# A hybrid encoder block in fp32 halves: one shared ring of half pieces for landed weights, sums and low parts

## The chip, the cores and the metric

The kernel runs on one core of one Trainium2 chip. The metric is the device time of one execution in microseconds (us), as a median of several runs. A profiled execution gives the trace from which the rows below come.

## The reference, cut to what matters

One layer of an encoder on 256 tokens of width 2048, in fp32. `w_in` has 10240 columns, the MLP is 5632 wide.

```
h = rms_norm(x, attn_norm)
proj = h @ w_in                       # q, k, v of branch A; q, k, v of branch B; gates ga, gb
ya = windowed_gqa(qa, ka, va)         # 8 heads
yb = dilated_attention(qb, kb, vb)    # 12 heads in three patterns, merged to 4
merged = sigmoid(ga) * (ya @ w_branch_a) + sigmoid(gb) * (yb @ w_branch_b)
x = x + merged @ w_out
hf = rms_norm(x, ffn_norm)
g = dwconv_centred(hf @ w_ffn_gate, conv_w, conv_b)      # three taps over the tokens
x = x + (gelu(g) * (hf @ w_ffn_up)) @ w_ffn_down
x = x + sigmoid(rms_norm(x, ple_norm) @ w_ple_gate) * (p @ w_ple_proj)
out = rms_norm(x, final_norm)
```

## The kernel before, in words

All weights lie in HBM as pieces of 128 x 2048 fp32 (1 MB), in the order of use: 258 pieces. Each product is done to nearly fp32 precision in parts: a weight `w` is rounded to a high part `hi` (ScalarE, a copy to the type fp32r, L264) and a low part `lo = w - hi` (VectorE, L265), the activations likewise, and TensorE multiplies the parts. `block` and `unit_blocks` (L292, L308 and L293, L315) have the weights as the stationary operand: a matmul of 512 columns with `hi` (both parts of the activations side by side) and one of 256 columns with `lo`. `thirds` (L365 to L367) has the activations stationary and three matmuls of 512 columns.

A *unit* is the part of a piece that is rounded in one go, mostly half a piece (1024 columns). `produce` makes the next unit: it asks for the pieces up to two ahead (`load`, on SP's DMA queue, into the ring `raw` of three whole pieces), then rounds the unit. Units go into rings: six pairs `uh`, `ul`, and, for sums, two pairs `vh`, `vl`. When TensorE's last instruction on a unit is issued, `drop` frees it and `pump` produces more while a ring has room. A planner orders the instructions of each engine by its own costs and the order of the program; `keep` pins an instruction to the order of the program. Every buffer's reuse is a wait on whoever used it last.

The stages, in order: A (projections and attention: stationary weights), then for j = 0 to 3 the gates B*j* with the branch products `ba`*j* and `bb`*j*, D0 and D1 (`w_out`), E0 (gate and up of the first half of the MLP), F00 and F01 (its part of `w_ffn_down`), E1, F10 and F11, `pp0` and `pp1` (the embedding), and G0, G2, G3 (its gate). E is stationary weights; B, D, F and G0 are *quad stages*: two 512-column halves by two token halves by pairs of contraction chunks. A piece of a quad stage is `s` (eight products, each three matmuls) or `S`, in which seven products take the place of eight, as in Strassen's and Winograd's scheme: M1 to M7, on sums of the activations (`combos`, `sums_of`) and on four sums of the weights. For an `S` piece `produce` wrote the sums in place on the landed piece, with one VectorE operation of 1024 columns and two of 512 (L257 to L259), after both plain units had been rounded; the units `T13` and `T24` are the sums'. Patterns such as "SsSsSsSs" give the pieces of a stage. At the end of a quad stage `row_sums` adds the banks up (L823 to L826), and the residual rows are updated and squared (L936, L938, L940).

In stage E, `mlp` works on one chunk of 128 MLP columns at a time, as its accumulator ends: `gather` adds the two halves of the accumulator (L456, L460); for a gate chunk the norm, three taps and the gelu's polynomial and tanh (L981 to L989), for an up chunk the product with the gelu and the split into high and low parts (L995 to L997).

The last product, G3, is two pieces taken together (`joint`), and its last two contraction chunks of the second token half are done by halves of 256 columns (`ends`), so that the first half of the bank is complete earlier. Then come the rows' tanh, residual, squares and the final norm (L1106 to L1122), and the output's DMAs.

Of the kernel before, what the change touches and what calls it, by code (L numbers as in the profile page):

```python
# [10 lines left out]
F32 = mybir.dt.float32  # L11
FR = mybir.dt.float32r
AF = mybir.ActivationFunctionType
ALU = mybir.AluOpType
# [73 lines left out]
WARM = 11  # L88
JOINT = 4
JOINED = 2  # L90
# [8 lines left out]
def _ffn(half):  # L99

    jobs = []
    for f in range(FHALF + 1):
        if f < FHALF:
            jobs.append(("g", half * FHALF + f))
        if f:
            jobs.append(("u", half * FHALF + f - 1))
    return jobs
# [52 lines left out]
_PIECES, _STAGES = _pieces()  # L160
_NPIECES = len(_PIECES)
# [22 lines left out]
RINGS = {"u": 6, "v": 2}  # L184
# [3 lines left out]
def _encoder(ctx: ExitStack, tc, xt, pt, xrow, cols, gainrow, table, onehot, mask, ident_in, wts, out):  # L188
# [42 lines left out]
    def tap(i, f):  # L231
# [5 lines left out]
    raws, made = {}, {}  # L237
    state = {"raw": 0, "unit": 0, "at": 0, "early": True,
             "u": RINGS["u"], "v": RINGS["v"]}

    def load(r, a=0, b=PIECE):
        if a == 0:
            raws[r] = wpool.tile([P, PIECE * P], F32, name="raw", bufs=3)
        nc.sync.dma_start(raws[r][:, a * P:b * P], wts[r][:, a * P:b * P])
        state["raw"] = r + 1

    def produce():

        u = state["unit"]
        p, kind, a, b = _UNITS[u]  # L250
        while state["raw"] < min(p + 3, _NPIECES):
            load(state["raw"])
        raw = raws[p]
        ring = "u" if kind == "n" else "v"
        if kind == "T13":
            q = [raw[:, i * WIDE:(i + 1) * WIDE] for i in range(4)]
            nc.vector.tensor_tensor(raw[:, :2 * WIDE], raw[:, WIDE:3 * WIDE], raw[:, :2 * WIDE], op=ALU.subtract)  # L257
            nc.vector.tensor_tensor(q[2], q[2], q[0], op=ALU.subtract)
            nc.vector.tensor_tensor(q[3], q[3], q[2], op=ALU.subtract)  # L259
        src = raw[:, a:b]  # L260
        pool = wpool if ring == "u" else held["tok"]
        hi = pool.tile([P, b - a], FR, name=ring + "h", bufs=RINGS[ring])
        lo = pool.tile([P, b - a], FR, name=ring + "l", bufs=RINGS[ring])
        nc.scalar.activation(hi, src, AF.Copy)  # L264
        nc.vector.tensor_tensor(lo, src, hi.bitcast(F32), op=ALU.subtract)  # L265
        made[u] = (hi, lo)
        state["unit"] = u + 1
        state[ring] -= 1

    def pump():  # L270
        while not state["early"] and state["unit"] < len(_UNITS):
            p, kind = _UNITS[state["unit"]][:2]
            if state["u" if kind == "n" else "v"] <= 0 or kind != "n" and "tok" not in held:
                break
            produce()
# [6 lines left out]
    def drop(u):  # L282
        del made[u]
        state["u" if _UNITS[u][1] == "n" else "v"] += 1
        pump()
# [76 lines left out]
    def thirds(acc, stationary, w, first, last):  # L362

        (sh, sl), (wh, wl) = stationary, w
        nc.tensor.matmul(acc, sh, wh, start=first, stop=False, skip_group_check=True)  # L365
        nc.tensor.matmul(acc, sh, wl, start=False, stop=False, skip_group_check=True)  # L366
        nc.tensor.matmul(acc, sl, wh, start=False, stop=last, skip_group_check=True)  # L367
# [4 lines left out]
    def quad_stage(stage, moving, combos=None, tags=("M2", "M3", "M4", "P22")):  # L372
# [24 lines left out]
        for i, p in enumerate(pieces):  # L397
            kind = _PIECES[p][0]
            us = _UNITS_OF[p]
            a, b = moving(2 * i), moving(2 * i + 1)  # L400
            if kind == "s":
                for g in range(8):
                    run_due(stage, i, g)
                    t, n, c = g // 4, g // 2 % 2, g % 2
                    w = cut(us[c], n if c == 0 else 1 - n)
                    put(tags[2 * t + n], part((a, b)[c], t), w)
                drop(us[0])
                drop(us[1])
            else:
                s = combos(i)  # L410
                sums = [(s[:, 0, e], s[:, 1, e]) for e in range(4)]
                for g, (name, stationary, u, c, gone) in enumerate((
                        ("M1", part(a, 0), 0, 0, 0), ("M7", sums[2], 2, 1, None), ("M5", sums[0], 2, 0, 2),
                        ("M6", sums[1], 3, 0, None), ("M2", part(b, 0), 1, 1, None), ("M3", sums[3], 1, 0, 1),
                        ("M4", part(b, 1), 3, 1, 3))):
                    run_due(stage, i, g)
                    put(name, stationary, cut(us[u], c))
                    if gone is not None:
                        drop(us[gone])
        return accs  # L420

    def wide_stage(stage, moving, names, joint=1):
# [3 lines left out]
        ends = []  # L426
        alone = len(pieces) - joint
        for i, span in [(i, 1) for i in range(alone)] + [(alone, joint)]:
            g = 0
            for t in range(2):  # L430
                for c in range(4 * span):
# [11 lines left out]
            for h in range(2) if ends else ():  # L443
                for e, (stationary, w) in enumerate(ends):
                    cs = slice(h * T, (h + 1) * T)
                    thirds(accs[1][:, cs], stationary, [a[:, cs] for a in w], False, e == 1)
            if ends:
                drop(_UNITS_OF[pieces[-1]][1])
# [84 lines left out]
    tot = ap_.tile([P, T], F32, name="tot", bufs=1)  # L533
# [11 lines left out]
    for step in order:  # L545
        if len(step) == 3:
            load(*step)
        elif step[0]:
            cs = slice(KC + step[0] * T, KC + step[1] * T)
            nc.sync.dma_start(flat[:, cs], xt[:, cs])  # L550
    nc.sync.dma_start(cl, cols)
    nc.sync.dma_start(ident, ident_in)
    nc.sync.dma_start(oh, onehot)
    nc.sync.dma_start(tb, table)
    nc.sync.dma_start(mk, mask)
# [13 lines left out]
    for step in order:  # L569
# [9 lines left out]
        while 4 * done + 5 < state["at"] // FIRST:  # L579
            square(done)  # L580
            done += 1
# [4 lines left out]

    for i in range(2):
        first_gather(i)
# [384 lines left out]

    def mlp(kind, n, acc):
        tok = held["tok"]
        if kind == "g":
            if n % 2 == 0:
                held["gw"] = tok.tile([P, 4, T], F32, name="gw", tag="c%d" % (n // 2 % 2 + 1))
            c, w = (held["gw"][:, 2 * (n % 2) + i] for i in range(2))
            u = gather(acc)  # L980
            nc.vector.tensor_tensor(u, u, rt[1], op=ALU.mult)  # L981
            nc.vector.tensor_scalar(c, u, tap(1, n), tap(3, n), op0=ALU.mult, op1=ALU.add)
            nc.vector.scalar_tensor_tensor(c[:, 1:], u[:, :-1], tap(0, n), c[:, 1:], op0=ALU.mult, op1=ALU.add)
            nc.vector.scalar_tensor_tensor(c[:, :-1], u[:, 1:], tap(2, n), c[:, :-1], op0=ALU.mult, op1=ALU.add)
            nc.scalar.activation(w, c, AF.Square)
            nc.vector.tensor_scalar(w, w, 0.044715, 1.0, op0=ALU.mult, op1=ALU.add)
            nc.vector.tensor_tensor(w, w, c, op=ALU.mult)
            nc.scalar.activation(w, w, AF.Tanh, scale=GELU_C)
            nc.vector.scalar_tensor_tensor(c, w, 1.0, c, op0=ALU.add, op1=ALU.mult)  # L989
            held["gelu", n] = c  # L990
        else:
            if n % 2 == 0:
                held["pair"] = tok.tile([P, 2, T], F32, name="pair", bufs=2)
            u = gather(acc, u=held["pair"][:, n % 2])
            nc.vector.scalar_tensor_tensor(u, u, 0.5, rt[1], op0=ALU.mult, op1=ALU.mult)  # L995
            nc.vector.tensor_tensor(u, u, held.pop(("gelu", n)), op=ALU.mult)
            halves(activation_row(n), u)  # L997
            pair = n % FHALF // 2
            if n % 2 and DOWN[pair] == "S":
                combos["act", pair] = sums_of(held["pair"], pair // 2)  # L1000
# [101 lines left out]
    for t in range(2):  # L1102
# [8 lines left out]
        nc.vector.tensor_tensor(known[:, t:t + 1], known[:, t:t + 1], ssq[:, t, 3:4], op=ALU.add)  # L1111
        nc.vector.tensor_scalar(v, ssq[:, t, 4:], known[:, t:t + 1], 1.0 / D, op0=ALU.add, op1=ALU.mult)
        r = sc.tile([P, 1], F32, name="r3")
        nc.gpsimd.tensor_tensor(r, v, mhalf[:, :1], op=ALU.pow)
        nc.vector.tensor_tensor(xr[:, t, cut[3]], xr[:, t, cut[3]], gains[:, cut[3]], op=ALU.mult)
# [62 lines left out]
```

## Time and profile before

| | |
|---|---|
| median of 3 runs | 1457.39 us (1457.05 to 1457.96) |
| the profiled execution: its own time | 1457.96 us |
| its span from first to last instruction | 1456.2 us |
| TensorE matmul busy | 1444.5 us, 7488 matmuls |
| VectorE (DVE) busy | 1248.8 us |
| ScalarE (ACT) busy | 822.1 us |
| HBM read | 279.49 MB, 193 GB/s over the span |

In the rows, PE is TensorE's matmuls, PEld its weight loads (they run beside matmuls), DVE VectorE, ACT ScalarE, POOL GpSimd, SP the engine that issues most DMAs. A row of a group has the line, engine, operation, written and read tiles, shapes and count, then busy us, mean ns of one, and the engine's idle time just before. A row of the timeline begins with start and length in us, and ends, where the engine had waited, with for how long and on whom. Matmuls overlap, so the length of one (391 ns for 512 columns) is more than the distance to the next.

### The profile page before, as it was taken

How to read it: one execution, taken by the hardware profiler on the slowest of the kernel's cores; microseconds unless marked ns; L12 is line 12 of the kernel's file. 1: busy time of each engine (PE TensorE's matmuls, PEld its weight loads, DVE VectorE, ACT ScalarE, POOL GpSimd, SP SyncE). 2: the span in 40 equal slices, each digit the busy share in tenths (PEclk: the TensorE clock that was granted, in tenths of full speed). 3: DMA queues.
4: the chain of work that ended last, by engine and by line, in shares of the span. 5: the costliest groups of instructions: out<-in, count | busy, mean ns of one | idle time of the engine just before them, and what ended most of it. 6: DMA issues, size and time to landing. Idle time of an engine off the chain costs nothing.

```text
span 1456.2 us, 19520 instructions
## 1 busy us (share of the span) xinstructions
PE 1444.5 (99%) x7488; PEld 1235.9 (85%) x7488; DVE 1248.8 (86%) x1849; ACT 822.1 (56%) x1141; POOL 4.1 (0%) x9
## 2 busy tenths in 40 slices
PE   9999999999999999999999999999999999999997
PEld 8888888888888888888888888888888888888785
DVE  7677665679998989989888899989888889999995
ACT  7455544446555656666555555455555555565762
POOL 0000000000000000000000000000000000000000
PEclk9999999999999999999999999999999999999999
DMA  9654444535546456465554545565555554546462
GB/s 335 249 206 146 152 168 175 175 141 203 192 187 235 180 213 234 174 232 193 186 199 175 202 152 221 176 254 183 199 184 193 185 192 173 193 191 234 170 237 81
DMA packets 46312, 282.88 MB, mean 194 GB/s; under 512 B 4932, under 2 KB 9668, under 8 KB 13964
## 3 DMA queue, kind: packets, MB, share of 16 engines
q1 hardware_dynamic: 45500, 280.46, 53.2%
q8 instruction: 58, 0.95, 0.3%
q10 hardware_dynamic: 720, 1.19, 0.2%
q14 instruction: 34, 0.28, 0.1%
HBM read 279.49 MB, written 2.14 MB: 193 GB/s over the span
## 4 chain that ended last, share of the span: by engine, by line
PE 97%; DVE 1%; ACT 1%; issue 1%; DMA 0%; SPq 0%; POOL 0%; POOLq 0%; DVEq 0%; ACTq 0%
PE bank L308 29%; PE bank L315 15%; PE bank L365 14%; PE bank L366 14%; PE bank L367 14%; PE bank L354 2%; PE bank L356 2%; PE bank L355 2%; PE bank L292 1%; PE bank L293 1%; PE bank L870 1%; PE bank L687 0%; PE bank L635 0%; PE bank L634 0%; PE bank L633 0%
## 5 line engine op out<-in xcount | busy, mean ns | idle before, releaser
L264 ACT ACTIVATE uh<-raw 128x1024 fp32r<-128x1024 f32 (+2 forms) x518 | 522.3, 1017 | 399.5 <-PE bank L308 183.6
L265 DVE TENSOR_TENSOR ul<-raw,uh 128x1024 fp32r<-128x1024 f32 (+2 forms) x518 | 596.8, 1169 | 128.9 <-ACT uh L264 68.8
L308 PE MATMUL bank<-hf,uh 128*128 128x512 f32 x1408 | 336.3, 391 | 0.0
L308 PEld LDWEIGHTS bank<-hf,uh 128*128 128x128 f32 x1408 | 258.9, 188 | 50.2
L315 PEld LDWEIGHTS bank<-hf,ul 128*128 128x128 f32 x1408 | 180.4, 191 | 6.7
L315 PE MATMUL bank<-hf,ul 128*128 128x256 f32 x1408 | 182.8, 283 | 0.0
L264 ACT ACTIVATE vh<-raw 128x1024 fp32r<-128x1024 f32 x92 | 97.4, 1058 | 57.0 <-DVE raw L257 25.4
L265 DVE TENSOR_TENSOR vl<-raw,vh 128x1024 fp32r<-128x1024 f32 x92 | 111.9, 1219 | 0.4
L308 PE MATMUL bank<-hs,uh 128*128 128x512 f32 x432 | 103.6, 392 | 0.0
L456 ACT ACTIVATE t<-bank 128x256 f32<-128x256 f32 x122 | 46.5, 384 | 96.6 <-PE bank L315 89.5
L308 PEld LDWEIGHTS bank<-hs,uh 128*128 128x128 f32 x432 | 79.5, 188 | 15.6
L365 PE MATMUL bank<-uh,act 128*128 128x512 f32 x232 | 90.4, 390 | 0.0
L366 PE MATMUL bank<-ul,act 128*128 128x512 f32 x232 | 90.4, 390 | 0.0
L367 PE MATMUL bank<-uh,act 128*128 128x512 f32 x232 | 90.3, 389 | 0.0
L365 PE MATMUL bank<-uh,hs 128*128 128x512 f32 x172 | 67.3, 391 | 0.0
L367 PE MATMUL bank<-uh,hs 128*128 128x512 f32 x172 | 67.3, 391 | 0.0
L366 PE MATMUL bank<-ul,hs 128*128 128x512 f32 x172 | 67.1, 390 | 0.0
L257 DVE TENSOR_TENSOR raw<-raw 128x1024 f32<-128x1024 f32 x46 | 56.1, 1221 | 0.6
L315 PE MATMUL bank<-hs,ul 128*128 128x256 f32 x432 | 56.6, 284 | 0.0
L315 PEld LDWEIGHTS bank<-hs,ul 128*128 128x128 f32 x432 | 54.5, 191 | 1.0
L366 PE MATMUL bank<-vl,S 128*128 128x512 f32 x138 | 54.1, 392 | 0.1
L365 PE MATMUL bank<-vh,S 128*128 128x512 f32 x138 | 54.1, 398 | 0.0
(240 smaller groups left out, 2273.2 us busy)
## 6 DMA issues: line engine op xcount, KB each, us to landing
raw<-in_wts SPq DMA_DIRECT2D x251, 1024.0 KB, 4.8
raw<-in_wts SPq DMA_DIRECT2D x12, 512.0 KB, 7.2
xr<-in_xrow SPq DMA_DIRECT2D x4, 512.0 KB, 8.3
x<-in_xt SPq DMA_DIRECT2D x13, 128.0 KB, 6.0
hb<-hold SPq DMA_DIRECT2D x3, 514.0 KB, 5.9
hb<-hold SPq DMA_DIRECT2D x2, 768.0 KB, 7.5
last<-in_gainrow SPq DMA_DIRECT2D x1, 1024.0 KB, 6.9
out<-xr SPq DMA_DIRECT2D x4, 256.0 KB, 2.6
```

The lines of the kernel that those rows point to most:

```text
L257: nc.vector.tensor_tensor(raw[:, :2 * WIDE], raw[:, WIDE:3 * WIDE], raw[:, :2 * WIDE], op=ALU.subtract)
L264: nc.scalar.activation(hi, src, AF.Copy)
L265: nc.vector.tensor_tensor(lo, src, hi.bitcast(F32), op=ALU.subtract)
L308: nc.tensor.matmul(acc, weights(u)[0][:, o * P:(o + 1) * P], m, start=first, stop=False, skip_group_check=True)
L315: nc.tensor.matmul(acc[:, T:], weights(u)[1][:, o * P:(o + 1) * P], m[:, :T], start=False, stop=last, skip_group_check=True)
L354: nc.tensor.matmul(acc[:, :n * P], xh, hi, start=(k == 0), stop=False)
L355: nc.tensor.matmul(acc[:, :n * P], xh, lo, start=False, stop=False)
L356: nc.tensor.matmul(acc[:, :n * P], xl, hi, start=False, stop=(k == KC - 1))
L365: nc.tensor.matmul(acc, sh, wh, start=first, stop=False, skip_group_check=True)
L366: nc.tensor.matmul(acc, sh, wl, start=False, stop=False, skip_group_check=True)
L367: nc.tensor.matmul(acc, sl, wh, start=False, stop=last, skip_group_check=True)
L456: keep(nc.scalar.activation(t, acc[:, T:], AF.Copy, scale=scale))
```

## The change

- The rings `raw`, `uh`/`ul` and `vh`/`vl` go. One ring `w` of twelve tiles of 128 x 1024 (`SPLIT`) holds landed half pieces, the sums of weights, and low parts; a ring `h` of seven (`ROUND`) holds the high parts. Each load is half a piece; `produce` asks for four loads beyond those that it needs (`AHEAD`).
- An `S` piece's units are ordered: first half's plain columns, both units of sums, second half's. Its sums are written by four operations of 512 columns into two tiles of the ring, before its first unit is rounded. M4 is moved ahead of M2 and M3. Code for sums kept in DRAM (`_SUMS_AT`, kind `Z`) is added, and is not used: `_SUMS_AT` is empty.
- `mlp` evacuates each chunk as before, but does everything after that for two chunks at a time, on tiles of 512 columns; the centre tap goes to ScalarE, and the up product of a chunk comes two gate products later instead of one (`LAG`).
- At the start the loads and the chunks of `x` are asked for twelve steps ahead of their use (`EARLY`), not all at once; the squares come four chunks later; `tot` shares the slot of `far`.
- G3 is no longer cut in halves. Three instructions of the last norm are kept in the order of the program.

The core of the diff:

```diff
-    for f in range(FHALF + 1):
+    for f in range(FHALF + LAG):                       # LAG = 2
...
-        elif kind == "S":
-            cuts = [("n", 0, WIDE), ("n", 2 * WIDE, 4 * WIDE), ("T13", 0, 2 * WIDE), ("T24", 2 * WIDE, 4 * WIDE)]
+        elif kind in "SZ":
+            cuts = [("n", 0, WIDE), (kind + "13", 0, 2 * WIDE), (kind + "24", 2 * WIDE, 4 * WIDE),
+                    ("n", 2 * WIDE, 4 * WIDE)]
...
-RINGS = {"u": 6, "v": 2}
+SPLIT, ROUND = 12, 7
+AHEAD = 4
...
+    def load():
+        u, p, half = _LOADS[state["load"]]
+        state["load"] += 1
+        t = wpool.tile([P, 2 * WIDE], F32, name="w", bufs=SPLIT)
...
+        nc.sync.dma_start(t[:, :b - a], src[:, a:b])
+
+    def sums_of_weights(p):
...
+        t, v = (wpool.tile([P, 2 * WIDE], F32, name="w", bufs=SPLIT) for _ in range(2))
...
+        nc.vector.tensor_tensor(s1, q[1], q[0], op=ALU.subtract)
+        nc.vector.tensor_tensor(s2, q[2], s1, op=ALU.subtract)
+        nc.vector.tensor_tensor(s3, q[2], q[1], op=ALU.subtract)
+        nc.vector.tensor_tensor(s4, q[3], s2, op=ALU.subtract)
...
     def produce():
...
-        while state["raw"] < min(p + 3, _NPIECES):
-            load(state["raw"])
...
+        last = us[-1] if _PIECES[p][0] == "S" else u
+        while state["load"] < min(_LOAD_OF[last] + 1 + AHEAD, len(_LOADS)):
+            load()
+        if u == us[0]:
...
+            if _PIECES[p][0] == "S":
+                sums_of_weights(p)
...
+        hi = wpool.tile([P, 2 * WIDE], FR, name="h", bufs=ROUND)[:, :n]
+        lo = wpool.tile([P, 2 * WIDE], FR, name="l", tag="w", bufs=SPLIT)[:, :n]
+        nc.scalar.activation(hi, w, AF.Copy)
+        nc.vector.tensor_tensor(lo, w, hi.bitcast(F32), op=ALU.subtract)
...
-                        ("M1", part(a, 0), 0, 0, 0), ("M7", sums[2], 2, 1, None), ("M5", sums[0], 2, 0, 2),
-                        ("M6", sums[1], 3, 0, None), ("M2", part(b, 0), 1, 1, None), ("M3", sums[3], 1, 0, 1),
-                        ("M4", part(b, 1), 3, 1, 3))):
+                        ("M1", part(a, 0), 0, 0, 0), ("M7", sums[2], 1, 1 - z, None), ("M5", sums[0], 1, z, 1),
+                        ("M6", sums[1], 2, 0, None), ("M4", part(b, 1), 2, 1, 2),
+                        ("M2", part(b, 0), 3, 1, None), ("M3", sums[3], 3, 0, 3))):
...
-                    if 1 < joint == span and t and c >= 4 * span - 2:
-                        ends.append((part(moving(k), t), w))
-                        continue
...
-        while 4 * done + 5 < state["at"] // FIRST:
+        while 4 * done + 9 < state["at"] // FIRST:
             square(done)
...
     def mlp(kind, n, acc):
...
+            gather(acc, u=g[:, k])
+            if k == 0:
+                return
+            nc.vector.tensor_tensor(g, g, both(rt[1]), op=ALU.mult)
+            for i in range(2):
+                f = n - 1 + i
+                nc.scalar.activation(c[:, i], g[:, i], AF.Identity, scale=tap(1, f), bias=tap(3, f))
+                nc.vector.scalar_tensor_tensor(c[:, i, 1:], g[:, i, :-1], tap(0, f), c[:, i, 1:],
+                                               op0=ALU.mult, op1=ALU.add)
+                nc.vector.scalar_tensor_tensor(c[:, i, :-1], g[:, i, 1:], tap(2, f), c[:, i, :-1],
+                                               op0=ALU.mult, op1=ALU.add)
+            nc.scalar.activation(g, c, AF.Square, scale=math.sqrt(0.044715))
+            nc.vector.scalar_tensor_tensor(g, g, 1.0, c, op0=ALU.add, op1=ALU.mult)
+            nc.scalar.activation(g, g, AF.Tanh, scale=GELU_C)
+            nc.vector.scalar_tensor_tensor(c, g, 1.0, c, op0=ALU.add, op1=ALU.mult)
...
-        nc.vector.tensor_tensor(known[:, t:t + 1], known[:, t:t + 1], ssq[:, t, 3:4], op=ALU.add)
-        nc.vector.tensor_scalar(v, ssq[:, t, 4:], known[:, t:t + 1], 1.0 / D, op0=ALU.add, op1=ALU.mult)
+        keep(nc.vector.tensor_tensor(known[:, t:t + 1], known[:, t:t + 1], ssq[:, t, 3:4], op=ALU.add))
+        keep(nc.vector.tensor_scalar(v, ssq[:, t, 4:], known[:, t:t + 1], 1.0 / D, op0=ALU.add, op1=ALU.mult))
...
-        nc.vector.tensor_tensor(xr[:, t, cut[3]], xr[:, t, cut[3]], gains[:, cut[3]], op=ALU.mult)
+        keep(nc.vector.tensor_tensor(xr[:, t, cut[3]], xr[:, t, cut[3]], gains[:, cut[3]], op=ALU.mult))
```

More of the change, by code (lines that the diff above doesn't have):

```diff
@@ L88 @@
 WARM = 11
+EARLY = 12
 JOINT = 4
+LAG = 2
 JOINED = 2
@@ L234, in _encoder @@
     sinks = cl[:, 3 * KC + 4 * FC:]
[L237 to L245, printed above, removed]
+    raws, made, sums_in = {}, {}, {}
+    state = {"load": 0, "unit": 0, "at": 0, "early": True, "free": ROUND}
@@ L283, in drop @@
         del made[u]
[L284 removed]
+        state["free"] += 1
         pump()
@@ L544, in _encoder, with ask @@
         chunk = need
[L545 to L555, printed above, removed]
+    asked = [0]
+    def ask(n):
+        for step in order[asked[0]:n]:
+            if len(step) == 3:
+                load()
+            elif step[0]:
+                cs = slice(KC + step[0] * T, KC + step[1] * T)
+                nc.sync.dma_start(flat[:, cs], xt[:, cs])
+        asked[0] = max(n, asked[0])
+        if n >= len(order) and "asked" not in held:
+            held["asked"] = True
+            nc.sync.dma_start(cl, cols)
+            nc.sync.dma_start(ident, ident_in)
+            nc.sync.dma_start(oh, onehot)
+            nc.sync.dma_start(tb, table)
+            nc.sync.dma_start(mk, mask)
     squares = ap_.tile([P, 4, T], F32, name="squares", tag="s3", bufs=1)
@@ L568, in _encoder @@
     ready = done = 0
-    for step in order:
+    for i, step in enumerate(order):
+        ask(i + EARLY)
         if len(step) == 3:
@@ L972, in activation_row, with both @@
         return held["act"][1][k - 16] if 16 <= k < 20 else held["act"][k // 20 * 2][:, k - k // 20 * 20, :]
+    def both(a):
+        return view(a, 0, (0, 2), (1, T))
     def mlp(kind, n, acc):
-        tok = held["tok"]
+        tok, k = held["tok"], n % 2
         if kind == "g":
[L977 to L989, printed above, removed]
```

117 lines of the change are left out of this document (79 added, 38 removed).

## The prediction

> **What bounds the kernel now.** I read the page first: who is busy, and what the chain that ended last is made of.
>
> ```profile
> span 1456.2 us, 19520 instructions
> ...
> PE 1444.5 (99%) x7488; PEld 1235.9 (85%) x7488; DVE 1248.8 (86%) x1849; ACT 822.1 (56%) x1141; POOL 4.1 (0%) x9
> ...
> PE 97%; DVE 1%; ACT 1%; issue 1%; DMA 0%; SPq 0%; POOL 0%; POOLq 0%; DVEq 0%; ACTq 0%
> ```
>
> The chain is TensorE for 97%, so only fewer or denser matmuls, or the remaining 3%, can move the end. A busy matmul row is not yet a matmul at its pitch, so the second view is the pitch along the chain in order of time.
>
> ```profile
> 60.44 3.65 PE bank L308 x16
> 64.09 1.91 PE bank L315 x16
> ```
>
> Sixteen 512-column matmuls start 228 ns apart (3.65/16), sixteen 256-column ones 119 ns apart. The third view asks whether that pitch holds everywhere.
>
> ```profile
> 13.00:47.00 34.00, 34.00 (x191) 28.69 (x190) 27.04 (x35) 23.00 (x32) 0.00 (x0) 1.00 0.81 304
> ...
> 425.00:467.00 42.00, 42.00 (x190) 34.38 (x189) 39.68 (x48) 23.86 (x27) 0.00 (x0) 1.00 0.62 238
> ...
> 584.00:608.00 24.00, 24.00 (x113) 19.35 (x112) 23.24 (x32) 15.84 (x23) 0.00 (x0) 1.00 0.44 170
> ...
> 700.00:875.00 175.00, 175.00 (x1012) 154.86 (x1011) 154.21 (x272) 97.33 (x146) 0.00 (x0) 1.00 0.52 184
> ```
>
> The columns are length, busy time and count of PE, PEld, DVE, ACT and POOL, granted clock, DMA share, GB/s. In the MLP stretch (700 to 875) 1012 matmuls, half of each width, take 173 ns each, the mean of 228 and 119: no gap. In the quad stage B2 (425 to 467) 190 matmuls take 221 ns each: no gap either. The clock is 1.00. The fourth view is what the weight loads, one step ahead of the matmuls, waited for.
>
> ```profile
> PEld bank L365 <- ACT vh L264: 1.1, 3, 0.4
> ...
> PEld bank L366 <- DVE vl L265: 0.8, 2, 0.5
> ...
> PEld bank L292 <- ACT uh L264: 0.2, 1, 0.2
> ```
>
> There are 14 such rows, from 1.1 us down to 0.2 us, 9.0 us together. That is all a better weight feed could return, an upper bound, since a waiting load is partly covered by the running matmul. So the change is about 9 us at the head and middle, the stretch after the last matmul, and whatever new waits it brings.
>
> **The change, part by part.**
>
> *Last product (G3) no longer cut in halves, and three instructions kept in order at the end.*
>
> ```profile
> 1445.64 0.28 PE L367 MATMUL bank<-uh,pl 128*128 128x256 f32 x1
> 1446.32 0.84 ACT L1106 ACTIVATE c<-bank,rh 128x256 f32<-128x256 f32 x2 [0.97 <-PE bank L367]
> ...
> 1448.90 0.15 DVE L1111 TENSOR_TENSOR known<-known,ssq 128x1 f32<-128x1 f32 x1
> 1449.01 0.69 DVE L1115 TENSOR_TENSOR xr<-xr,last 128x512 f32<-128x512 f32 x1
> 1449.62 0.21 DVE L1112 TENSOR_SCALAR v<-ssq,known 128x1 f32<-128x1 f32 x1
> 1449.91 0.55 POOL L1114 TENSOR_TENSOR r<-v,mhalf 128x1 f32<-128x1 f32 x1 [5.32 <-DVE v L1112]
> 1450.50 0.72 ACT L1119 ACTIVATE xr<-xr,r 128x512 f32<-128x512 f32 x1 [3.33 <-POOL r L1114]
> 1450.50 1.28 DVE L1121 TENSOR_SCALAR xr<-xr,r 128x512 f32<-128x512 f32 x3 [0.67 <-POOL r L1114]
> ```
>
> In the source L1112 stands ahead of L1115, in the trace behind it. Kept in order, L1112 starts where L1115 started, at 1449.01 instead of 1449.62; POOL's power and the last scaling follow 0.61 us earlier. L1115's 0.69 us then lies beside the 0.88 us from L1112's start to the scaling, so it costs nothing. Twelve half-width matmuls become six: 11 steps of 119 ns and 0.28 us (1.59 us) against 5 of 228 ns and about 0.39 us (1.53 us), minus 0.06. Nothing is lost with the halves: both activations of the last bank (x2 at 1446.32) came after the whole of it. Sum: minus 0.67, bounds minus 0.9 and 0.
>
> *First products: requests in steps (EARLY), squares four chunks later, `tot` in the slot of `far`.*
>
> ```profile
> 9.41 1.04 ACT L562 ACTIVATE squares<-x 128x1024 f32<-128x1024 f32 x1
> 10.36 1.04 ACT L264 ACTIVATE uh<-raw 128x1024 fp32r<-128x1024 f32 x1
> ...
> 12.71 0.41 PEld L293 LDWEIGHTS bank<-hs,ul 128*128 128x128 f32 x3 [0.73 <-DVE ul L265]
> ...
> 44.12 0.73 ACT L456 ACTIVATE t<-bank 128x256 f32<-128x256 f32 x2 [5.42 <-PE bank L293]
> 44.53 0.77 DVE L460 TENSOR_TENSOR first<-bank,t 128x256 f32<-128x256 f32 x2 [4.58 <-ACT t L456]
> ```
>
> The square stands ahead of the rounding whose low part the weight load at 12.71 awaits for 0.73 us. Without it the rounding can start up to 0.95 us sooner, if its data have landed; I take minus 0.3, bounds minus 0.7 and plus 0.7. The two squares left over cost nothing: ACT sits idle for 5.42 us and DVE for 4.58 us before the first evacuation; were that cover gone, 2 x 1.04 us of ACT from 44.85 would still end before 47. SP is asked for the same transfers in the same order, nothing on it is moved past a needed one.
>
> *MLP activations by pairs, LAG 2.*
>
> ```profile
> L995 DVE SCALAR_TENSOR_TENSOR pair<-pair,rms 128x256 f32<-128x256 f32 x44 | 18.7, 426 | 1.2
> ...
> L986 DVE TENSOR_SCALAR gw<-gw 128x256 f32<-128x256 f32 x44 | 12.6, 286 | 0.0
> ...
> L985 ACT ACTIVATE gw<-gw 128x256 f32<-128x256 f32 x44 | 17.7, 403 | 0.4 <-DVE gw L984 0.3
> ```
>
> For two chunks 16 DVE operations of 286 to 426 ns (4.6 to 6.8 us) become six of double width, 4.1 us at the 686 ns of L258 below; the four tap operations stay and the centre tap goes to ACT, two more of about 403 ns. DVE saves 0.5 to 2.7 us for each of 22 pairs, 11 to 59 us. Its worth is nothing: in that stretch DVE already idles 21 of 175 us, ACT 78, and no matmul waits. Each accumulator is still evacuated at once.
>
> *Sums into tiles of their own, M4 moved ahead of M2 and M3, one ring.*
>
> ```profile
> L257 DVE TENSOR_TENSOR raw<-raw 128x1024 f32<-128x1024 f32 x46 | 56.1, 1221 | 0.6
> ...
> L258 DVE TENSOR_TENSOR raw<-raw 128x512 f32<-128x512 f32 x46 | 31.5, 686 | 0.4
> L259 DVE TENSOR_TENSOR raw<-raw 128x512 f32<-128x512 f32 x46 | 31.5, 685 | 0.2
> ```
>
> An S piece had 1221 + 686 + 685 = 2592 ns of sums; four 512-wide ones are 2744: plus 0.15 us for 46 pieces, 7 us of DVE, all in quad stages, where DVE is busy 39.68 of 42 us. Hidden as long as the weights are ahead. How far ahead they are is read from when a low part is written and when TensorE first reads it:
>
> ```profile
> 441.05 1.22 DVE L265 TENSOR_TENSOR vl<-raw,vh 128x1024 fp32r<-128x1024 f32 x1
> ...
> 447.89 0.39 PE L366 MATMUL bank<-vl,S 128*128 128x512 f32 x1
> ...
> 593.28 1.22 DVE L265 TENSOR_TENSOR vl<-raw,vh 128x1024 fp32r<-128x1024 f32 x1
> ...
> 594.97 0.40 PE L366 MATMUL bank<-vl,S 128*128 128x512 f32 x1
> ```
>
> In B2 the sums' low part is ready 5.6 us early (442.27 to 447.89); in D1, loaded with the rows' work of the stage before it, 0.5 us.
>
> With the change, before an S piece's first unit is rounded six halves must be asked for (its two and four ahead) and two sums made: eight of twelve slots, four for low parts. Seven low parts are never there in an S stage. The second sum tile comes free when the piece before it, also S, has dropped its first sum unit, after three products, 9 x 0.228 = 2.0 us in. Sums 2.74, then 0.69 and 1.22 of low parts: M7's weights stand at 6.7 us, and are needed 45 + 3 matmuls (10.9 us) in. The lead is 4.2 us against 5.6: minus 1.4. In its favour, the second half-piece's low part (1.22 us) no longer comes ahead of the sums, M4 frees its unit six matmuls sooner, and M2, M3 come last: where DVE is the limit, as in D1, M7's weights come 1.22 - 0.15 = 1.1 us sooner. In D1 that makes 0.5 - 1.4 + 1.1 = 0.2 us: just enough. The same meeting of rows' work and S pieces comes in F01, F11 and G0. I take 0; bounds minus 2 (the waits on vh and vl above) and plus 6 (four places at 1.4). A late low part would next hold the evacuations that are issued behind it on DVE.
>
> *Loads in halves.*
>
> ```profile
> raw<-in_wts SPq DMA_DIRECT2D x251, 1024.0 KB, 4.8
> raw<-in_wts SPq DMA_DIRECT2D x12, 512.0 KB, 7.2
> ```
>
> 251 whole pieces become about 502 halves, at SP nothing that TensorE sees. Halves in flight four deep at the loaded 7.2 us give 4 x 0.524 MB / 7.2 us = 291 GB/s; the fastest stage asks 238, the start moved 304. Cost 0 with thin cover. The Trainium skill, "DMA: Bandwidth & Descriptors", section Bandwidth, speaks against it: batch transfers to 1 MiB or more for 75% of peak, with a fit of 2.0 us plus bytes over 436 GB/s. By that one half at a time would give an estimated 164 GB/s, and B2's 10 MB an estimated 61 us instead of 42; the 304 GB/s of the start, mostly halves, disagrees.
>
> **Sum.** 0.67 + 0.3 + 0 = 0.97 us less than the profiled execution's own 1457.96 us (span 1456.2 and 1.8 around it), which was 0.57 above the median of 1457.39. So about 1456.4 as a median.
>
> **Rivals.** *The ring starves the S pieces* (slower): the two sum tiles and the lookahead loads leave four low parts, and the lead of 4.2 us is used up by rows' work. It decides where a stage's S pieces come in less than 1.4 us before need today. For: D1 has 0.5 us. Against: the 1.1 us credit. Price: 1.4 us at four to six stage starts, less the 0.97 gained, plus 5 to 7: about 1462; were all 46 S pieces to lose 0.3 us, 1470. *All waits go* (faster): DVE's relief and the new order take half of the 9.0 us of weight waits besides the tail: 1457.4 - 0.7 - 4.5 = 1452.2. Against: the relief lies in the MLP, which has no waits. *Halves become the bound*: if only two are in flight, 146 GB/s, B2's 10 MB take 68 us instead of 42, over some ten quad stages plus 260: 1717. *The change does nothing*: the end keeps its order, 1457.4.
>
> **How the numbers follow.** Small gain or nothing, within 0.2% (2.9 us, about what a measurement of this kernel can tell from no change): 0.62, its own range 1454.6 to 1460.2. Starved S pieces 0.21, of which half beyond 1462. All waits go 0.15. Halves 0.02. Faster 0.16, same 0.61, slower 0.23. The range reaches from 1453.5 to 1463.0 and leaves out a tenth on each side.
>
> **What would show it.** Right: L1112 ahead of L1115 and about 0.6 us less between the last matmul and the end; the chain still TensorE for 97%; the MLP stretch the same length with DVE idle twice as long; D1 as long as before within 0.5 us. Wrong: weight loads waiting for DVE low parts by several us in D1, F01, F11 or G0; SP or ACT waiting for DMA in the quad stages; DVE waiting for slots that PE frees while evacuations stand behind it.

## The result, and the profile after

The changed kernel takes 1472.91 us (median of 4 runs; the kernel before beside it 1457.68): slower by 0.99%, ratio 1.0099 [1.0079, 1.0119]. In a second measurement it took 1471.55 us, ratio 1.0096 [1.0081, 1.0111]. The first measurement's profile fell on an execution that took 1801 us at a granted clock of 0.751 (the other three took 1471.01 to 1473.84, and the ratio goes by them), so the rows of "after" are those of the second measurement, whose execution took 1471.2 us (span 1469.4). 1456.4 us was forecast, at most 1463.0: the change cost 14 to 15 us where a gain of 1 us was forecast.

The page of after, its busy line, the chain, and the loads:

```profile
PE 1448.2 (99%) x7482; PEld 1236.9 (84%) x7482; DVE 1206.9 (82%) x1679; ACT 833.2 (57%) x1123; POOL 4.7 (0%) x9
...
PE 96%; DVE 2%; ACT 1%; issue 1%; DMA 0%; SPq 0%; POOLq 0%; POOL 0%; DVEq 0%; ACTq 0%
...
w<-in_wts SPq DMA_DIRECT2D x514, 512.0 KB, 4.6
```

VectorE has 42 us less to do, as meant, and the kernel is slower: DVE's share of the chain has gone from 1% to 2%, in whole per cents. Its busy share says nothing of that. Where it happens, the windows say. First the kernel before, then after, cut where the first matmul with a low part of a stage's weights starts: stage A, D1, E0 (and, of after, ten us within D1).

```profile
6.00:305.00 299.00, 298.71 (x1722) 262.62 (x1722) 206.93 (x317) 164.60 (x263) 1.02 (x1) 1.00 0.57 201
584.20:631.60 47.40, 47.39 (x215) 37.85 (x214) 45.71 (x56) 29.67 (x37) 0.00 (x0) 1.00 0.58 210
631.60:875.20 243.60, 243.60 (x1413) 215.56 (x1412) 216.02 (x390) 139.13 (x215) 0.71 (x1) 1.00 0.53 187
```

```profile
6.00:308.40 302.40, 299.76 (x1721) 263.42 (x1722) 210.33 (x319) 166.37 (x264) 1.02 (x1) 0.99 0.60 199
587.70:641.40 53.70, 48.83 (x209) 37.91 (x208) 46.27 (x57) 31.73 (x40) 0.00 (x0) 0.97 0.58 185
610.00:620.00 10.00, 7.13 (x23) 5.06 (x24) 4.84 (x8) 5.61 (x9) 0.00 (x0) 0.83 0.03 8
641.40:887.50 246.10, 245.23 (x1417) 216.42 (x1416) 195.57 (x289) 146.02 (x206) 0.70 (x1) 1.00 0.56 185
```

By these cuts A ends 3.6 us later (at 308.41, before at 304.81), D1 takes 6.3 us more, E0 2.5; F11 0.9 and G0 1.25 more, `pp0` with `pp1` 0.8 less, the end 0.4 less, all other stages stay within 0.3. Within 0.2 us that makes the 13.2 us between the spans. In D1, 4.87 us of the 6.3 are an idle TensorE (53.70 - 48.83), the rest is longer matmuls: the granted clock of 610 to 620 is 0.83. In E0 0.87 us are an idle TensorE; the other 1.6, at a granted clock of 1.00, were not taken apart. From 610 to 620 DMA moves 8 GB/s, since SP waits for a slot to ask with: its longest wait for VectorE's low parts, which free the landed halves that they read, lasts from 604.3 to 618.6.

```profile
SPq L276 <- DVE l L328: 515.9, 194, 14.3
```

*The start*, in the timeline of before (one row) and then of after:

```profile
5.33 1.21 DVE L265 TENSOR_TENSOR ul<-raw,uh 128x384 fp32r<-128x384 f32 x2
```

```profile
8.56 0.89 ACT L523 ACTIVATE hs<-x 128x256 fp32r<-128x256 f32 x2
9.09 0.88 DVE L524 SCALAR_TENSOR_TENSOR hs<-x,hs 128x256 fp32r<-128x256 f32 x2 [1.89 <-ACT hs L523]
9.89 1.15 DVE L328 TENSOR_TENSOR l<-w,h 128x384 fp32r<-128x384 f32 x2
...
10.49 1.82 PE L353 MATMUL bank<-hs,l 128*128 128x256 f32 x7 [2.62 <-DVE l L328]
```

The first low part is begun at 9.89, behind four chunks of `hs`; in the kernel before it was begun at 5.33, behind one, and read at 5.95. TensorE stands still for 2.62 us, and the granted clock of 12 to 20 is 0.85.

*D1*, VectorE alone, after, then (a kernel of the experiments, r4) with the sums in tiles of their own:

```profile
604.57 1.23 DVE L328 TENSOR_TENSOR l<-w,h 128x1024 fp32r<-128x1024 f32 x1
...
606.70 0.68 DVE L286 TENSOR_TENSOR w<-w 128x512 f32<-128x512 f32 x1
...
608.93 0.69 DVE L289 TENSOR_TENSOR w<-w 128x512 f32<-128x512 f32 x1
609.53 0.48 DVE L524 SCALAR_TENSOR_TENSOR hf<-bank,cl,hf 128x256 fp32r<-128x256 f32 x1
611.50 0.48 DVE L524 SCALAR_TENSOR_TENSOR hf<-bank,cl,hf 128x256 fp32r<-128x256 f32 x1 [1.50 <-ACT hf L523]
613.30 0.48 DVE L524 SCALAR_TENSOR_TENSOR hf<-bank,cl,hf 128x256 fp32r<-128x256 f32 x1 [1.32 <-ACT hf L523]
614.33 0.48 DVE L524 SCALAR_TENSOR_TENSOR hf<-bank,cl,hf 128x256 fp32r<-128x256 f32 x1 [0.54 <-ACT hf L523]
616.02 0.69 DVE L328 TENSOR_TENSOR l<-w,h 128x512 fp32r<-128x512 f32 x1 [1.21 <-PE bank L426]
```

```profile
598.00 0.70 DVE L286 TENSOR_TENSOR sw<-w 128x512 f32<-128x512 f32 x1
...
602.01 0.68 DVE L289 TENSOR_TENSOR sw<-w,sw 128x512 f32<-128x512 f32 x1
602.61 2.50 DVE L328 TENSOR_TENSOR l<-sw,h 128x1024 fp32r<-128x1024 f32 x2
605.03 0.48 DVE L527 SCALAR_TENSOR_TENSOR hf<-bank,cl,hf 128x256 fp32r<-128x256 f32 x1
605.42 1.21 DVE L328 TENSOR_TENSOR l<-w,h 128x1024 fp32r<-128x1024 f32 x1
```

L286 to L289 are the four sums of the third S piece. In r4 they begin 14.4 us into D1 (598.00, D1 from 583.62), and low parts follow the last one (L289) at once. After the change they begin 19.0 us into D1 (606.70, D1 from 587.68), and no low part is written for 10.2 us, from 605.80 to 616.02: behind the last sum VectorE does four evacuations of 0.48 us, three of which wait for ScalarE's half of the same work (ACT `hf`), and the next low part itself waits 1.21 us for a matmul with a low part (L426) to give back its slot. ScalarE and TensorE at the same time:

```profile
609.11 2.00 ACT L327 ACTIVATE h<-w 128x1024 fp32r<-128x1024 f32 x2
...
610.21 0.73 PE L425 MATMUL bank<-h,S 128*128 128x512 f32 x2 [0.97 <-ACT h L327]
611.02 0.45 ACT L523 ACTIVATE hf<-bank,cl 128x256 fp32r<-128x256 f32 x1
...
614.96 0.60 PE L425 MATMUL bank<-h,merged 128*128 128x512 f32 x1 [2.20 <-DVE hf L524]
615.36 0.63 PE L426 MATMUL bank<-l,merged 128*128 128x512 f32 x1
615.78 0.63 PE L427 MATMUL bank<-h,merged 128*128 128x512 f32 x1
616.21 0.63 PE L425 MATMUL bank<-h,merged 128*128 128x512 f32 x1
```

ScalarE rounds the late sums first (609.11) and does its half of the next evacuation behind them (611.02). TensorE waits for the sums' high parts, and then for the evacuations. All of its 4.87 us in D1 are such waits: 1.81 for high parts (ACT `h`), 2.44 for evacuations (DVE `hf`), 0.62 for a residual row (DVE `xr`); none is for a low part. The low part at 616.02 in turn needs a slot that a matmul behind the longest of these waits gives back. So it is a loop through three engines, and the rows of this one place do not say which link of it is first to be late; the experiments below change the slots.

The matmuls behind the wait start 425 ns apart instead of 228, until 618.4: about 1.5 us more.

### The profile page after: what moved, and what is told of

Same layout as the page of the kernel before. It is cut to its first block, busy times and chain, and to the rows that moved or that the text cites. A ratio compares the mean times of both kernels' runs of the same rounds, so it can differ in the third digit from the quotient of the medians.

```text
span 1799.2 us, 20185 instructions
## 1 busy us (share of the span) xinstructions
PE 1782.0 (99%) x7482; PEld 1349.7 (75%) x7482; DVE 1222.2 (68%) x1679; ACT 835.4 (46%) x1123; POOL 4.7 (0%) x9
## 4 chain that ended last, share of the span: by engine, by line
PE 98%; issue 0%; DVE 0%; ACT 0%; DMA 0%; SPq 0%; POOLq 0%; POOL 0%; DVEq 0%; ACTq 0%
PE bank L368 29%; PE bank L425 15%; PE bank L427 15%; PE bank L426 14%; PE bank L375 14%; PE bank L414 2%; PE bank L416 2%; PE bank L415 2%; PE bank L352 2%; PE bank L353 1%; PE bank L929 1%; PE bank L746 0%; PE bank L694 0%; PE bank L693 0%; PE bank L692 0%
## 5 line engine op out<-in xcount | busy, mean ns | idle before, releaser
L328 DVE TENSOR_TENSOR l<-w,h 128x1024 fp32r<-128x1024 f32 (+2 forms) x610 | 709.8, 1178 | 361.4 <-ACT h L327 200.8
L327 ACT ACTIVATE h<-w 128x1024 fp32r<-128x1024 f32 (+2 forms) x610 | 610.7, 1021 | 696.8 <-PE bank L368 259.7
L368 PE MATMUL bank<-hf,h 128*128 128x512 f32 x1408 | 415.6, 455 | 0.1
L368 PEld LDWEIGHTS bank<-hf,h 128*128 128x128 f32 x1408 | 273.8, 199 | 106.5 <-DVE hf L524 0.9
L375 PEld LDWEIGHTS bank<-hf,l 128*128 128x128 f32 x1408 | 211.5, 212 | 14.6 <-issue 0.2
L375 PE MATMUL bank<-hf,l 128*128 128x256 f32 x1408 | 215.4, 316 | 0.0
L368 PE MATMUL bank<-hs,h 128*128 128x512 f32 x432 | 127.9, 458 | 0.0
L427 PE MATMUL bank<-h,act 128*128 128x512 f32 x252 | 115.4, 459 | 0.0
L426 PE MATMUL bank<-l,act 128*128 128x512 f32 x252 | 114.9, 456 | 0.0
L425 PE MATMUL bank<-h,act 128*128 128x512 f32 x252 | 114.3, 455 | 0.0
L425 PE MATMUL bank<-h,hs 128*128 128x512 f32 x186 | 85.3, 459 | 0.0
L426 PE MATMUL bank<-l,hs 128*128 128x512 f32 x186 | 85.2, 458 | 0.0
L427 PE MATMUL bank<-h,hs 128*128 128x512 f32 x186 | 84.9, 457 | 0.0
L425 PE MATMUL bank<-h,S 128*128 128x512 f32 x184 | 83.7, 460 | 0.8 <-ACT h L327 0.7
L426 PE MATMUL bank<-l,S 128*128 128x512 f32 x184 | 83.9, 456 | 0.0
L427 PE MATMUL bank<-h,S 128*128 128x512 f32 x184 | 83.7, 456 | 0.0
L425 PEld LDWEIGHTS bank<-h,act 128*128 128x128 f32 x252 | 50.4, 200 | 21.2 <-issue 0.4
L426 PEld LDWEIGHTS bank<-l,act 128*128 128x128 f32 x252 | 50.2, 199 | 21.1
```

The source lines that it names most:

```text
L327: nc.scalar.activation(hi, w, AF.Copy)
L328: nc.vector.tensor_tensor(lo, w, hi.bitcast(F32), op=ALU.subtract)
L368: nc.tensor.matmul(acc, weights(u)[0][:, o * P:(o + 1) * P], m, start=first, stop=False, skip_group_check=True)
L375: nc.tensor.matmul(acc[:, T:], weights(u)[1][:, o * P:(o + 1) * P], m[:, :T], start=False, stop=last, skip_group_check=True)
L425: nc.tensor.matmul(acc, sh, wh, start=first, stop=False)
L426: nc.tensor.matmul(acc, sh, wl, start=False, stop=False)
```

## The experiments

Four theories. *Start*: tiles of one ring are handed out in the order of the program; with twelve steps asked for at once, the first low part's tile comes behind seven loads, and so do its rounding and its reader. *Slots*: a piece of sums wants two tiles more than before from a ring that the loads beyond the need have filled. *Order*: not the number of slots but their handing out starves the low parts. *Halves or pairs*: smaller loads or the new `mlp` cost something.

**r1, the changed kernel again.**

> The changed kernel itself, for a trace at the full clock. Theory P (places): its 15 us lie in two places, the first low part at the start (about 3.4 us of waiting in the throttled trace) and the second S piece of D1 (about 4 us), each followed by some microseconds of matmuls at a lower granted clock: weight loads wait for DVE low parts at 7 us and for DVE and ACT near 600 us, and the other quad stages have the length of before within 0.3 us each. Theory R (the ring starves all S pieces, 0.3 us each): the 15 us are spread over the 11 quad stages, 1 to 1.5 us in each, and the start is as before. Both: 1471 to 1474 us.

1471.55 us (1470.99 to 1471.96). Its rows are shown above. TensorE's waits for data in D1 and behind it are for DVE `hf`, `pl`, `xr` and ACT `h`, none for DMA and none for a low part. Neither theory holds as it stands: the start and D1 lose 9.9 us, but E0, F11 and G0 lose 4.7 more, and the other quad stages nothing.

**r2, loads asked for six steps ahead at the start.**

```diff
-EARLY = 12
+EARLY = 6
```

> The changed kernel with EARLY = 6 in place of 12: the seventh load is asked for after the first low part's tile, not before it. Theory O (slots of the shared ring are handed out in the order of the program, so the planner puts the first two low parts behind the seventh load and three chunks of hs on DVE): the low part at the start comes at about 5.3 us again, the 3.4 us wait there goes and with it the slow matmuls behind it; 1466 to 1469 us against 1472. Theory D (the start waits for data, the loads in halves land later): the wait stays, 1471 to 1474.

1467.42 us, ratio to the kernel before 1.0064 [1.0047, 1.0080]: 4.1 less than r1. The first low part is read at 7.48 instead of 10.49, and A ends at 304.10 (after: 308.41; before: 304.81). D1 and E0 stay at 54.2 and 246.1. The start's loss is settled: it came with the step of the requests. That the planner puts the low part behind the seventh load because of the order of the tiles is the theory's reading; r9 below bears on it.

**r3, the sums in two tiles of their own**, in the pool `tok`, which is open only behind stage A.

```diff
-        t, v = (wpool.tile([P, 2 * WIDE], F32, name="w", bufs=SPLIT) for _ in range(2))
+        t, v = (held["tok"].tile([P, 2 * WIDE], F32, name="sw", bufs=2) for _ in range(2))
...
+            p = _UNITS[state["unit"]][0]
+            if _PIECES[p][0] == "S" and "tok" not in held:
+                break
```

> The changed kernel with the two tiles of sums of weights of an S piece in a ring of two of their own and not among the twelve (the twelve then hold six landed halves and six low parts at an S piece). Theory P/R (slots are what the S pieces lack): D1's waits of about 4 us go, 1465 to 1468 us if D1 is the place, 1460 to 1463 if all S pieces lose. Rival M (the order of the products, M4 ahead, or the pace of DVE, makes D1 late): no change, 1471 to 1474.

1459.71 us, ratio 1.0018 [1.0008, 1.0028]: 11.8 less than r1. D1 46.65, E0 243.73, F11 57.93, G0 41.22: all of the loss behind A is gone, more than either theory expected. The start remains (2.5 us of wait at one place).

**r4, both edits.**

> Both edits: sums of weights in a ring of their own and EARLY = 6. Theory P with O: both losses go, 1456 to 1460 us, level with the kernel before or a microsecond under it by the shorter tail. If something else costs (halves at SP, pairs in the MLP), 1462 to 1470.

1455.71 us (1455.16 to 1456.79, 10 runs), ratio 0.9988 [0.9978, 0.9997]: level with r7 the fastest kernel of the study, by little, and within the 0.2% of the kernel before that was called about what a measurement can tell. Its waits of TensorE for data, complete:

```profile
PE bank L245 <- DVE mhalf L240: 1.1, 1, 1.1
PE bank L356 <- DVE l L328: 1.0, 2, 0.6
PE bank L355 <- DVE hs L527: 0.2, 1, 0.2
```

The loads are halves here too and E has the pairs: neither costs anything that shows.

**r5, two loads beyond the need instead of four** (on r2).

```diff
-AHEAD = 4
+AHEAD = 2
```

> The sums back in the shared ring, requests in steps of six as in r2, and AHEAD 2 instead of 4: beside a piece of sums two of the twelve slots no longer hold data that are wanted only later. If it is the number of slots that starves the low parts, most of what r2 has over r4 goes (D1 54.2 us towards 46.7 to 48, E0 246.1 towards 243.7): 1456 to 1461 us. Rival: the sums are late because they share a ring in program order with the loads, however many slots are spare, or because the second sum waits for its own predecessor: 1466 to 1469, D1 above 53. A third: loads only two halves ahead are late themselves, slower than 1469 with low or high parts waiting for DMA.

1461.52 us, ratio 1.0026 [1.0016, 1.0036]. D1 50.0, E0 244.7, F11 58.5: 5.9 of the 11.7 us between r2 and r4 come back, with no more memory; that is 0.5 us above the range of the theory of slots, and D1 stays above its 48. Two spare slots are worth that much and do not do it all, and B1 to D0 lose 0.2 to 0.3 us each.

**r6, M4 back behind M2 and M3** (on r4).

```diff
-                        ("M6", sums[1], 2, 0, None), ("M4", part(b, 1), 2, 1, 2),
-                        ("M2", part(b, 0), 3, 1, None), ("M3", sums[3], 3, 0, 3))):
+                        ("M6", sums[1], 2, 0, None), ("M2", part(b, 0), 3, 1, None),
+                        ("M3", sums[3], 3, 0, 3), ("M4", part(b, 1), 2, 1, 2))):
```

> r4 (sums apart, requests in steps of six) with the fourth product put back behind M2 and M3. The prediction credited the move with 1.1 us in D1 and nothing elsewhere. If D1 is still just in time, D1 grows from 46.65 by 0.5 to 1.5 us and the total goes to 1456.2 to 1457.5. If sums in tiles of their own give D1 slack, nothing changes: 1455.2 to 1456.2. If the move costs something elsewhere it becomes faster, 1454 to 1455.

1456.09 us, ratio 0.9988 [0.9979, 0.9997], as r4. D1 46.61 against 46.65: the move is worth nothing where slots suffice. What it is worth in the full ring was not tried.

**r7, `mlp` chunk by chunk and LAG 1, as before** (on r4).

> r4 with the MLP's activations chunk by chunk and LAG 1, as in the kernel before. The prediction gave the pairs no worth, because no matmul of E waits: E0 243.7, E1 241.5, total 1455.2 to 1456.2, DVE busy 20 to 60 us more. Rival: DVE's relief is what lets the rounding run ahead into F00 and F10, then those stages lose 0.5 us or more each: 1457 to 1460.

1455.64 us, ratio 0.9987 [0.9979, 0.9996]: no difference. E1 takes 241.51 us in the kernel before, after, r4 and here; the pairs take some 26 us of work from VectorE in it and give nothing.

**r8, without the three instructions kept in order** (on r4).

```diff
-        keep(nc.vector.tensor_tensor(known[:, t:t + 1], known[:, t:t + 1], ssq[:, t, 3:4], op=ALU.add))
-        keep(nc.vector.tensor_scalar(v, ssq[:, t, 4:], known[:, t:t + 1], 1.0 / D, op0=ALU.add, op1=ALU.mult))
+        nc.vector.tensor_tensor(known[:, t:t + 1], known[:, t:t + 1], ssq[:, t, 3:4], op=ALU.add)
+        nc.vector.tensor_scalar(v, ssq[:, t, 4:], known[:, t:t + 1], 1.0 / D, op0=ALU.add, op1=ALU.mult)
...
-        keep(nc.vector.tensor_tensor(xr[:, t, cut[3]], xr[:, t, cut[3]], gains[:, cut[3]], op=ALU.mult))
+        nc.vector.tensor_tensor(xr[:, t, cut[3]], xr[:, t, cut[3]], gains[:, cut[3]], op=ALU.mult)
```

> r4 without the three instructions kept in order at the end. Theory: the order goes back to the scaling by the gains ahead of the mean, POOL's power takes about 0.55 us again instead of 0.93, and the end comes 0.33 us later: 1456.0 us, from the last matmul to the end 10.2 to 10.3 us instead of 9.94. Rival: the planner keeps the new order by itself: 1455.7 and 9.94 us.

1456.11 us, ratio 0.9990 [0.9981, 0.9999]; from the last matmul to the end 10.16 us against 9.94, so the order is worth 0.22. First the last norm of r8, then of r1:

```profile
1447.45 0.69 DVE L1196 TENSOR_TENSOR xr<-xr,last 128x512 f32<-128x512 f32 x1
1448.06 0.21 DVE L1193 TENSOR_SCALAR v<-ssq,known 128x1 f32<-128x1 f32 x1
1448.35 0.55 POOL L1195 TENSOR_TENSOR r<-v,mhalf 128x1 f32<-128x1 f32 x1 [5.31 <-DVE v L1193]
```

```profile
1462.56 0.21 DVE L1190 TENSOR_SCALAR v<-ssq,known 128x1 f32<-128x1 f32 x1
1462.69 0.68 DVE L1193 TENSOR_TENSOR xr<-xr,last 128x512 f32<-128x512 f32 x1
1462.85 0.93 POOL L1192 TENSOR_TENSOR r<-v,mhalf 128x1 f32<-128x1 f32 x1 [4.79 <-DVE v L1190]
```

Kept in order, the mean `v` comes first, and POOL's power takes 0.93 us beside VectorE's multiplication instead of 0.55 alone. Of the 0.61 us forecast, 0.38 are given back.

**r9, low parts first**: the same ring and number, but a unit takes its tiles before the four loads beyond its need are asked for (on r2).

```diff
-        while state["load"] < min(_LOAD_OF[last] + 1 + AHEAD, len(_LOADS)):
+        while state["load"] < _LOAD_OF[last] + 1:
             load()
...
         made[u] = (hi, lo)
+        while state["load"] < min(_LOAD_OF[last] + 1 + AHEAD, len(_LOADS)):
+            load()
```

> The sums in the shared ring and steps of six as in r2, but each unit takes the slots of its high and low part before the four loads beyond its need are asked for, not after. Number of slots and memory stay the same, only the order in which slots are handed out changes. If the order is the cause, the start comes down to the kernel before's (first low part read at about 6 us instead of 7.5) and D1 with E0 loses most of its 9.4 us: 1455 to 1460 us. If in D1 the number is the cause (AHEAD 2 returned about half), only the start changes: 1464 to 1467.

1461.00 us, ratio 1.0020 [1.0011, 1.0030], between both expectations. D1 50.4, E0 244.2. VectorE's waits ahead of the low parts, of r1 and then of r9:

```profile
DVE l L328 <- issue: 78.4, 39, 2.7
DVE l L328 <- ACT h L327: 45.0, 34, 2.7
DVE l L328 <- PE bank L375: 18.6, 21, 3.1
```

```profile
DVE l L328 <- ACT h L327: 157.3, 152, 2.9
```

The waits for TensorE's slots are gone from the view's upper rows, and low parts wait for their high parts nearly alone. These sums go over the whole run and do not say where time was lost: r4, which has no stall in D1, has the three waits too, at 68.9, 60.4 and 19.1 us. The times do say it: the order of handing out carries part of the loss, 6.4 of the 11.7 us. 3.8 us of D1 stay. At the start the first low part is read at 6.21 instead of 7.48, as the theory of order has it, but A ends no earlier (304.55 against 304.10).

**r10, ten tiles in the ring and two for the sums** (on r4): twelve again.

```diff
-SPLIT, ROUND = 12, 7
+SPLIT, ROUND = 10, 7
```

> r4 with ten tiles in the shared ring: with the two tiles of the sums again twelve, the memory of the change as it was made. If sums need tiles that nobody else can hold, whatever the number of the others, this stays at r4's 1455 to 1457 us (D1 46.7). If r4 is fast because it has fourteen tiles, it goes back towards r2: D1 50 to 54, 1460 to 1467.

1474.37 us, ratio 1.0115 [1.0102, 1.0129], slower than the change itself, and beyond the 1467 expected at most: D1 53.8, and B2 (43.75), F10 (57.9) and F11 (61.0) lose 1.4 to 3 us each as well.

```profile
PE bank L429 <- DVE l L328: 2.9, 6, 1.1
PE bank L428 <- DVE hf L527: 2.2, 1, 2.2
```

So r3 and r4 are fast because they have fourteen tiles behind stage A; standing apart alone does not do it. Fourteen tiles in one ring were not tried.

**r11, r4 with the low parts first.**

> r4 (sums apart, steps of six) with the slots of high and low parts taken before the four loads beyond the need, as in r9. r4's D1 and E0 have no stall left, so only the start can gain: first low part read at 7.2 us in r4, 5.95 in the kernel before. Expect 0.5 to 1.3 us less than r4: 1454.2 to 1455.3. Rival: the loads, asked for later, are late somewhere, 1456 or more.

1459.10 us, ratio 1.0011 [1.0002, 1.0020]: slower than r4 by 3.4. The first low part is read at 6.34 instead of 7.21, and A ends at the same time (304.56 against 304.63); E0 takes 1.6 us more, B2 to D0 0.3 to 0.5 each. That is the rival's case: with enough slots, loads asked for later only lose here.

**r12, the sums written over the landed halves, as before** (on r2): two tiles less for each piece of sums, and both plain units are rounded ahead of the sums again.

```diff
-        t, v = (wpool.tile([P, 2 * WIDE], F32, name="w", bufs=SPLIT) for _ in range(2))
...
+        nc.vector.tensor_tensor(q[1], q[1], q[0], op=ALU.subtract)
+        nc.vector.tensor_tensor(q[2], q[2], q[1], op=ALU.subtract)
+        nc.vector.tensor_tensor(q[3], q[3], q[2], op=ALU.subtract)
+        nc.vector.tensor_tensor(q[0], q[2], q[0], op=ALU.subtract)
```

> r2 (one ring of twelve, steps of six) with the sums written over the landed halves, as in the kernel before, in four operations of 512 columns; a piece of sums then needs two slots less, with the memory of the change, but both plain units are rounded ahead of the sums again. If the two slots of the sums are what D1 and E0 lack, D1 goes from 54.2 us to 46.6 to 48 and the total to 1455 to 1459 us. If the late second sum comes from the order on VectorE (plain low parts first), D1 stays above 50 and the total is 1461 to 1468.

1500.63 us, ratio 1.0288 [1.0273, 1.0303]: a clear miss of both expectations. Each F stage loses 4.7 to 5.2 us, B2 3.6, D1 1.4 against r2. The timeline in F00:

```profile
915.04 0.69 DVE L283 TENSOR_TENSOR w<-w 128x512 f32<-128x512 f32 x1 [2.82 <-DMA w<-in_wts]
...
916.98 0.68 DVE L286 TENSOR_TENSOR w<-w 128x512 f32<-128x512 f32 x1
917.77 5.37 ACT L327 ACTIVATE h<-w 128x1024 fp32r<-128x1024 f32 x6 [7.65 <-DVE w L286]
...
918.88 0.50 PE L425 MATMUL bank<-h,S 128*128 128x512 f32 x1 [1.26 <-ACT h L327]
```

Here sums wait for their data (27.8 us in 19 waits over the run), ScalarE for the last sum, TensorE for ScalarE. One reading: a half holds its tile from its request until the sums in it are rounded, so the next load is asked for late. It is argued, not tested, and the order of the units, which went back in the same edit, is a rival that no run parts from it. Two tiles less for a piece did not help here.

## Why the prediction was wrong, point by point

**What bounds it**: right. The chain stayed TensorE, 96%; the loss is new waits and, in A and D1, the clock behind them (1.6 us of E0 were not taken apart).

**Sums in the shared ring: the step that failed.** The prediction put D1's lead at 0.2 us, "just enough", and took 0, between minus 2 and plus 6. Measured, D1 plus E0 are 8.9 us longer, F11 0.9 and G0 1.25: 11.0 in all. Of the four places that were named F01 lost nothing, and E0, which begins with rows that D1's VectorE finishes, was not in the list. "A late low part would next hold the evacuations" was near: in the rows of D1 the sums are late, ScalarE's rounding of them and its half of the evacuations come behind, and those hold TensorE; no matmul there waits for a low part.

Three things were mis-sized. The lead was counted for one piece by itself (eight of twelve slots, four left), but the loss is a loop: low parts wait for slots that TensorE gives back, landed halves stay until their low parts are made, and TensorE waits for work of ScalarE and VectorE that stands among the rounding. It made 10.2 us without a low part, not a lead shorter by 1.4. That slots are at the root of it is shown by r3, r5, r9 and r10, which change only how many there are, whose they are, or who gets them first; the links between are read from one place. E0 was left out. And a wait was priced at its own length; the clock added 1.5 us in D1. The 1.1 us credited to M4's new place, which had brought the lead back above zero, does not show where it was tried (r6: 0.04, in a kernel with slots to spare).

**The start: wrong in sign.** Minus 0.3 was taken, minus 0.7 to plus 0.7; A ended 3.6 us later. "SP is asked for the same transfers in the same order" was a sentence on the wrong thing: the new ring hands tiles to loads and to low parts in one sequence, and, as r2 and r9 bear out, the low part came behind loads that it had nothing to do with. r2 gave the loss back. Whether the gain that was forecast is there cannot be told: the kernels with requests six steps ahead and the same ring at the start (r2, r4, r6, r7, r8) end A between 304.10 and 305.11, the kernel before at 304.81.

**The tail: right in kind, half in size.** L1112's successor does stand first, but from the last matmul to the end 0.33 us came of 0.61, of which r8 gives 0.22 to the order, since POOL was slowed; the undivided G3 gave 0.07 for 0.06.

**MLP by pairs: 0, right** (r7); in E0 VectorE's idle time went from 27.6 to 50.5 us, nearly double. **Loads in halves: 0, right**: r4 asks for halves, and TensorE waits nowhere for DMA; nothing of the rival at 1717 us showed. The cover was read too large: the fastest stage of the kernel before asks 251 GB/s (608 to 632 us), not 238, against the 291 reckoned for four halves in flight. And the fit that the prediction quotes stands in another section of that page of the Trainium skill, "Anatomy of one DMA — SWDGE (gpsimd) path", for transfers that GpSimd issues; these are SP's.

**The rivals.** The starved ring was named with 0.21; its 1462 was too little, and its 1470 for "all 46" was reached through four places and the start. That part of the range's upper bound rested on 1.4 us a place, where D1 alone lost 6.3; for the start the bound was a loss of 0.7.

## What to carry to other kernels

When rings are merged, do not count only how many tiles a producer needs: write down the order in which the program hands them out, at the start and where two kinds of work share an engine, and ask who holds the tile that the next low part gets. A late producer on an in-order engine can cost more than its lateness, because other engines' work for TensorE, here the evacuations, comes late behind it; price a starved stage at the loop, not at the lead. Work taken from an engine that nobody waits for (42 us of VectorE here) is worth nothing, while two tiles (r10 against r4) were worth 19 us.

## What the runs showed of the hardware

*The clock after short waits.* In after, a longest single gap of 2.20 us, with others of 0.97, 0.22 and 0.24 us in the five us ahead of it, was followed by 3.4 us of matmuls 425 ns apart, and the granted clock of the ten us was 0.83. At the start waits of 0.78 and 2.62 us were followed by a granted clock of 0.85 from 12 to 20; behind the one wait of 0.87 us in E0 it stayed at 1.00. The Trainium skill, "TensorE: Matmul & The Clock Gate", section "What's actually happening", has the gate fall to half rate after an idle window of about 3.4 us: the half rate agrees with the rows (425 against 228 ns), but no single gap here was that long.

*POOL beside VectorE.* The power of a 128x1 tile took 0.93 us while VectorE multiplied two tiles in SBUF, 0.55 us alone (r1 and r8, above). The Trainium skill, "SBUF — State Buffer", section "SBUF: two separate sides", says that VectorE with two SBUF inputs and a GpSimd operation share a port pair, which one of them holds for its whole instruction. The rows agree that POOL is held up: it begins 0.16 us behind VectorE's start and loses 0.38 us; that the shared ports do it is the page's account.
